# Key pages, gate weights, adaLN pieces and value groups of a hybrid decoder step, moved to other stages

## The chip, the cores and the metric

The kernel runs on one core of a Trainium2 chip. The core has five engines that run their own instruction streams in order: TensorE (PE in the profile; PEld is its loading of weights), VectorE (DVE), ScalarE (ACT), GpSimd (POOL) and SyncE (SP), which here issues nearly all transfers. The metric is the device time of one launch in microseconds (us), lower is better.

## The reference

One layer of a decoder trunk for a prompt of 512 tokens and 8 samples of one new token each, 520 columns in all, with D = 1024, 16 heads of 64, a feed-forward width of 2816, in f32:

```python
m = adaLN(c)                      # shift1, scale1, gate1, shift2, scale2, gate2
h = RMSNorm(x) * (1 + scale1) + shift1
z = h @ w_in                      # rg_x | rg_gate | q | k | v | forget logits | gate A | gate B
ya = (rg_lru(conv4(rg_x)) * gelu(rg_gate)) @ w_proj_a
yb = attend(q, k, v, logf) @ w_proj_b
x = x + gate1 * ((sigmoid(gA) * ya + sigmoid(gB) * yb) @ w_o)
x = x + gate2 * SwiGLU(RMSNorm(x) * (1 + scale2) + shift2)
y = RMSNorm(x)
```

The prompt attends to itself; each sample attends to 1024 past tokens, which lie in 8 pages of 128 tokens per sample, found by a page table: 64 pages of keys and 64 of values, [128 tokens, 16 x 64] f32 each. The logits of the past are q . k / 8 plus a sum of log forget values; a softmax runs over them and the sample's own new token. The outputs are y, the new k, v and log forget values, and the states of the convolution and the recurrence.

## The kernel before

Activations lie with features on partitions: a tile is [128 features, 520 tokens], in two halves of 260 columns. Each f32 operand of a product is split into a rounded part and a rest (hi and lo, the latter the difference), and a product is three matmuls: hi x hi, lo x hi, hi x lo. For weights a chunk `wraw` (up to 1 MB, 2 buffers) is loaded by SP, ACT casts `whi` from it (L210), and DVE subtracts `wlo` (L211), with 3 buffers each, so the split units run ahead of PE by at most three. `begin` (L227) is called for each unit of 128 output features; it ticks the side work, loads chunks and splits weights as far ahead as a budget allows.

The stages in order: a start (RMSNorm, the first adaLN third, the first half of q); the **q stage**, one turn of a loop (L782) for each of q0 to q7; the **recurrent branch** (xr, ga, gb, gr: convolution, RG-LRU, gates); k0, v0 and the **projection pa**, eight units; eight **attention blocks**, each for two heads of the prompt (scores `sc`, softmax, transposes `ptt`, products `po`) with the k and v products of the next block; then pb, wo and the feed-forward part.

Side work is put between by hand-written tables. The units are numbered n = 0 (q6), 1 (q7), 2 and 3 (xr0, xr1), 4 and 5 (ga0, ga1), 6 and 7 (gb0, gb1) and so on; 33 ends the recurrent branch, and 41 ends pa.

- **Key pages.** `KEYS[n]` says how many pages unit n loads (L605 and L606: SP reads the page's number from the table, then issues the transfer into a buffer `pg`, of a pool that the adaLN weights `araw` and the row `qb` share). `qb` is a sample's q row, broadcast to all partitions from `qtd` in memory, where it was written after all q's transposes (`qt`, L763). Two ticks after a page's load DVE multiplies it by `qb` (L636) and sums over each head's 64 columns into `S` (L637); four pages (`POOL_KEYS`) are multiplied on POOL (L624). `KEYS` begins at n = 4 and gives 52 pages; 12 more come in attention blocks 0 to 2 (`KEYS_AT`).
- **The past's softmax** (`past_softmax`, L664 to L700) runs for each pair of samples, a step every two ticks, once its 16 pages are summed: maxima, `dg` (DVE), `lgm` (PE, L685), exponentials, `lgs` (PE).
- **Values** (`pv`, L718): a group is two value pages and four matmuls on PE. 8 groups are due in units of the recurrent branch and pa, 25 slots in attention.
- **Forget values**: POOL gathers the past's into `lfp`, which takes one of the two `wraw` buffers; `past_turn` transposes it (`lft`, PE), once after q6 and once after q7.
- **adaLN pieces** (`ada_piece`, L290): two transfers `araw` of 512 KB and four matmuls on PE each. Pieces 0 to 5 of the second third go with q2 to q7, 6 with xr0 and 7 with xr1.
- **Gate weights** of the RG-LRU (`gw`, `gws`, L823 to L857): loaded in `conv`, cast and subtracted behind each xr.
- **Decay rows** in attention (`decay_rows`): SP broadcasts a head's row `fb` from `ftd`; ACT copies half of it to `fm` (L1063), POOL adds a mask to the parts.

Of the kernel before, what the change touches and what calls it, by code (L numbers as in the profile page):

```python
# [8 lines left out]
F32 = mybir.dt.float32  # L9
F32R = mybir.dt.float32r  # L10
# [54 lines left out]
def kernel(ctx, tc, xT, par, gates, b_f, cst, cse, own, cache_k, cache_v, cache_lf, pt,  # L65
# [103 lines left out]
    def flush():  # L169
        while stores:  # L170
# [3 lines left out]

    KEYS = dict(zip(range(4, 42), (2, 2, 3, 2, 0, 0, 0, 1, 2, 2, 2, 1, 0, 0, 0, 1, 2, 2, 2, 2, 0, 1, 1, 1, 2, 2, 2, 3,
                                   1, 1, 2, 1, 2, 1, 2, 1, 2, 1)))
    VALUES = (21, 23, 25, 27, 29, 31, 35, 39)
    POOL_KEYS = (41, 44, 47, 50)
# [260 lines left out]
    def q_weights(fh, raw, ko, i):  # L439
# [5 lines left out]
        for k in range(0, 4, 2 if (fh, i) == (0, 0) else 4):  # L445
            ks = slice(k, k + 2 if (fh, i) == (0, 0) else 4)
            act.copy(hi[:, ks], src[:, ks])
            dve.tensor_tensor(lo[:, ks], src[:, ks], hi[:, ks].bitcast(F32), ALU.subtract)
        for n in range(2):
            qw[fh, i + n] = [(hi[:, k, 128 * n:128 * n + 128], lo[:, k, 128 * n:128 * n + 128]) for k in range(4)]  # L450

    def q_matmuls(fh, i, j, k, b):
        hi, lo = qw[fh, i][k]
        ah, al = h[4 * fh + k]
        t0, t1 = HALVES[j]
        for m, (wt, at) in enumerate(((hi, ah), (lo, ah), (hi, al))):
            pe.matmul(b[:, :HALF], lhsT=wt, rhs=at[:, t0:t1], start=k == 0 and m == 0, stop=k == 3 and m == 2)  # L457

# [141 lines left out]

    def page_load(cache, s, j):
        pg = pgp.tile([128, D], F32, name="pg", tag="pg")
# [10 lines left out]

    def key_page(s, j):
        if s == 0 and j == 0:
            S.extend(slot("S", 512) for _ in range(2))
        if j == 0:
            t = pgp.tile([128, D], F32, name="qb", tag="pg")
# [4 lines left out]
        if late:  # L623
            pool.tensor_tensor(pg, pg, qb[0], ALU.mult)  # L624
        pend.append([0, s, j, pg, None if late else qb[0]])

    def key_sums():
        for p in pend:
            p[0] += 1
        while pend and pend[0][0] >= 2:  # L630
            _, s, j, pg, q = pend.pop(0)
            r = s // 2
            c = 256 * (r % 2) + 32 * j + H * (s % 2)
            with tc.issue_after(state["last"].ins):
                if q is not None:
                    dve.tensor_tensor(pg, pg, q, ALU.mult)  # L636
                dve.tensor_reduce(S[r // 2][:, c:c + H], pg.rearrange("p (h d) -> p h d", d=DH), AX.X, ALU.add)  # L637
            summed[r] += 1
# [7 lines left out]

    keys_todo = [(s, j) for s in range(NS) for j in range(NPAGE)]
    chains = []
# [125 lines left out]
    def past_conv():  # L774
# [4 lines left out]
        dve.tensor_reduce(conv_past, t, AX.X, ALU.add)  # L779

    ready = []
    for i in range(KT):  # L782
# [15 lines left out]
        if i == 3:  # L798
            split_upto(0)
        if i == 4:  # L800
            past_load()
# [19 lines left out]

    gate_raw = {}

    def gate_load(i):
        if i not in gate_raw:
            gate_raw[i] = slot("gw", 256)
            sp.dma_start(gate_raw[i], gates[i])
        return gate_raw[i]

    def conv(i):  # L830
        gr = gate_load(i)
        if i + 1 < KT:
            gate_load(i + 1)
        xr, xc = slot("xr"), slot("xc")
# [19 lines left out]
        def close():  # L854
            gw = slot("gws", 512, F32R)
            act.copy(gw[:, :256], gr)
            dve.tensor_tensor(gw[:, 256:], gr, gw[:, :256].bitcast(F32), ALU.subtract)  # L857
            del gate_raw[i]
            lru[i].update(xs=split("xc", xc), gw=gw)

# [78 lines left out]
    for i in range(0, KT, 2):  # L939
        conv(i)  # L940
        if i == 0:
            q_done(*q_last)
            past_sums(0)
            ada_piece(1, 6)
        else:
            both(lru_root, i - 2)
            gelu(i - 2)
            lru_scan(i - 2)
        conv(i + 1)
        if i == 0:  # L950
            past_sums(1)
            ada_piece(1, 7)
            ada_copy(1)
        else:
            gelu(i - 1)
            lru_scan(i - 1)
            both(lru_mul, i - 2)
            both(lru_g, i - 2)
        if i < 6:
            gate_a(i)  # L960
            lru_gates(i)
            if i == 0:
                ada_end(1)
# [91 lines left out]
    def decay_rows(i):  # L1055
        for hd in (2 * i, 2 * i + 1):
# [5 lines left out]
            fm = slot("fm", 512)  # L1062
            act.copy(fm[:, :256], fb[:, :256])  # L1063
            for dst, b in ((f0[:, 128 * a:128 * a + 128], 0), (fm[:, 384:], 1), (fm[:, 256:384], 2), (fb[:, 384:], 3)):
# [469 lines left out]
```

## Time and profile before

| | us |
|---|---|
| median of 3 runs | 1085.18 (1083.56 to 1087.83) |
| the profiled execution's own time | 1084.21 |
| its span | 1082.1 |
| PE busy in the span | 1035.1 |
| q stage | 52 to 96 |
| recurrent branch | 96 to 296 |
| k0, v0 and pa | 296 to 369 |
| attention blocks | 369 to 585 |
| pb, wo, feed-forward part | 585 to 1082 |

Times inside the run are read from the trace of one profiled execution and count from the start of its span. Matmuls are pipelined: the 48 matmuls of a unit (two halves of 260 columns) take 5.96 us on PE's chain, though each single one is listed with 0.28. A row of the waits names the instruction that waited, what released it, the total, the number of times and the longest. A row of the chain gives start, duration, engine, result, line and count.

### The profile page before, as it was taken

The page shows a single profiled execution, that of the slowest core. Times are in us where ns is not written, and L with a number is a line of the kernel's source. Part 1 is how long each engine was busy: PE and PEld are TensorE (multiplying, and loading weights), DVE is VectorE, ACT ScalarE, POOL GpSimd, SP SyncE. Part 2 cuts the span into 40 slices and gives each one's busy share as a digit, 9 for nine tenths or more (in the row PEclk, how much of TensorE's full clock was granted, in tenths as well). Part 3 has the DMA queues.
Part 4 walks back from the last instruction along what each step waited for, and adds up shares of the span by engine and source line. Part 5 has one row for each costly group of instructions (what it writes and reads, how often), then busy time and mean ns, then how long its engine had stood idle before and what let it go on. Part 6 is the DMA issues. An engine that isn't in the chain of part 4 may idle for free.

```text
span 1082.1 us, 20877 instructions
## 1 busy us (share of the span) xinstructions
PE 1035.1 (96%) x8210; PEld 955.1 (88%) x8210; DVE 663.6 (61%) x1158; ACT 498.9 (46%) x983; POOL 161.3 (15%) x249
## 2 busy tenths in 40 slices
PE   4999999999979989998999999999999999999996
PEld 2888999999879967777778989999999999999995
DVE  5434799978899888875655455843343333433354
ACT  4423585857831466686775234533312332222352
POOL 1102010100032424452420002400000000000013
PEclk9999999999999989998999999999999999999998
DMA  9795776679779988898875773223323422323212
GB/s 335 264 346 197 237 268 188 213 247 294 245 220 334 295 282 248 288 295 267 237 248 194 256 278 86 72 79 81 115 78 88 109 79 95 101 79 99 77 60 80
DMA packets 164996, 206.94 MB, mean 191 GB/s; under 512 B 9490, under 2 KB 125730, under 8 KB 164834
## 3 DMA queue, kind: packets, MB, share of 16 engines
q1 hardware_dynamic: 161170, 198.70, 57.9%
q10 hardware_dynamic: 3648, 6.39, 1.6%
q8 instruction: 64, 1.05, 0.4%
q0 software_dynamic: 80, 0.52, 0.2%
q14 instruction: 34, 0.28, 0.1%
HBM read 192.49 MB, written 13.09 MB: 190 GB/s over the span
## 4 chain that ended last, share of the span: by engine, by line
PE 81%; DVE 7%; DMA 5%; ACT 2%; issue 2%; POOL 1%; SPq 1%; POOLq 0%; DVEq 0%
PE fiu L245 11%; PE fig L245 11%; PE fo L245 10%; PE gb L245 4%; PE xr L245 4%; PE pb L245 4%; PE ga L245 4%; PE v L245 4%; PE pa L245 3%; PE gr L245 3%; PE wo L245 3%; DMA fb<-ftd 2%; PE k L245 2%; PE pv L718 2%; PE qp L457 2%
## 5 line engine op out<-in xcount | busy, mean ns | idle before, releaser
L211 DVE TENSOR_TENSOR wlo<-wraw,whi 128x1024 fp32r<-128x1024 f32 (+1 forms) x131 | 163.1, 1245 | 161.3 <-ACT whi L210 161.3
L210 ACT CAST whi<-wraw 128x1024 fp32r<-128x1024 f32 (+1 forms) x131 | 136.4, 1041 | 209.3 <-PE fo L245 74.5
L245 PE MATMUL fiu<-h2h,whi 128*128 128x260 f32 x320 | 90.9, 284 | 0.0
L245 PE MATMUL fiu<-h2l,whi 128*128 128x260 f32 x320 | 90.6, 283 | 0.0
L245 PE MATMUL fig<-h2l,whi 128*128 128x260 f32 x320 | 90.3, 282 | 0.0
L245 PE MATMUL fiu<-h2h,wlo 128*128 128x260 f32 x320 | 90.3, 282 | 0.0
L245 PE MATMUL fig<-h2h,wlo 128*128 128x260 f32 x320 | 90.3, 282 | 0.0
L245 PE MATMUL fig<-h2h,whi 128*128 128x260 f32 x320 | 90.2, 282 | 0.0
L245 PE MATMUL fo<-ach,whi 128*128 128x260 f32 x292 | 82.7, 283 | 0.0
L245 PE MATMUL fo<-ach,wlo 128*128 128x260 f32 x292 | 82.5, 283 | 0.0
L245 PE MATMUL fo<-acl,whi 128*128 128x260 f32 x292 | 82.2, 282 | 0.0
L637 DVE TENSOR_REDUCE S<-pg 128x16 f32<-128x1024 f32 x64 | 76.4, 1210 | 1.3 <-POOL pg L624 1.0
L327 POOL TENSOR_TENSOR ss<-ss,sq 128x260 f32<-128x260 f32 x18 | 13.6, 757 | 420.3 <-ACT sq L326 419.8
L636 DVE TENSOR_TENSOR pg<-pg,qb 128x1024 f32<-128x1024 f32 x60 | 72.4, 1224 | 0.2 <-DMA pg<-in_cache_k_dram 0.2
L245 PEld LDWEIGHTS fiu<-h2h,wlo 128*128 128x128 f32 x320 | 60.5, 189 | 0.0
L245 PEld LDWEIGHTS fiu<-h2l,whi 128*128 128x128 f32 x320 | 60.3, 188 | 0.0
L245 PEld LDWEIGHTS fig<-h2h,whi 128*128 128x128 f32 x320 | 60.2, 188 | 0.0
L245 PEld LDWEIGHTS fig<-h2l,whi 128*128 128x128 f32 x320 | 60.2, 188 | 0.0
L245 PEld LDWEIGHTS fig<-h2h,wlo 128*128 128x128 f32 x320 | 60.2, 188 | 0.0
L245 PEld LDWEIGHTS fiu<-h2h,whi 128*128 128x128 f32 x320 | 60.2, 188 | 0.0
L245 PEld LDWEIGHTS fo<-acl,whi 128*128 128x128 f32 x292 | 55.0, 188 | 0.0
L245 PEld LDWEIGHTS fo<-ach,wlo 128*128 128x128 f32 x292 | 54.9, 188 | 0.0
(382 smaller groups left out, 3377.0 us busy)
## 6 DMA issues: line engine op xcount, KB each, us to landing
pg<-in_cache_k_dram SPq DMA_DIRECT2D x64, 512.0 KB, 5.3
pg<-in_cache_v_dram SPq DMA_DIRECT2D x64, 512.0 KB, 5.4
araw<-in_ada_w_dram SPq DMA_DIRECT2D x48, 512.0 KB, 7.3
wraw<-in_w_fi_dram SPq DMA_DIRECT2D x44, 512.0 KB, 5.1
wraw<-in_w_in_dram SPq DMA_DIRECT2D x34, 512.0 KB, 6.3
wraw<-in_w_in_dram SPq DMA_DIRECT2D x11, 1024.0 KB, 6.9
wraw<-in_w_fo_dram SPq DMA_DIRECT2D x8, 1024.0 KB, 5.3
x<-in_xT_dram SPq DMA_DIRECT2D x16, 260.0 KB, 6.2
```

The costliest lines, as they stand in the source:

```text
L210: state["act"] = act.copy(hi[:, :k1 - k0], src)
L211: state["last"] = dve.tensor_tensor(lo[:, :k1 - k0], src, hi[:, :k1 - k0].bitcast(F32), ALU.subtract)
L245: state["mm"] = pe.matmul(out[:, :HALF], lhsT=wt[k], rhs=at, start=k == 0 and m == 0, stop=k == nk - 1 and m == 2)
L327: eng.tensor_tensor(acc[:, t0:t1], acc[:, t0:t1], q_, ALU.add)
L457: pe.matmul(b[:, :HALF], lhsT=wt, rhs=at[:, t0:t1], start=k == 0 and m == 0, stop=k == 3 and m == 2)
L636: dve.tensor_tensor(pg, pg, q, ALU.mult)
L637: dve.tensor_reduce(S[r // 2][:, c:c + H], pg.rearrange("p (h d) -> p h d", d=DH), AX.X, ALU.add)
L718: pe.matmul(pv[0][32 * gq:32 * gq + 32, :], lhsT=pw[r][:, c:c + 32], rhs=pgs[gq // 2][:, 512 * hf:512 * hf + 512], start=j == 0, stop=j == ...
```

## The change

- Keys of samples 0 and 1 come as halves by heads: an item is a pair of pages, of each 512 of its 1024 columns (two transfers of 256 KB into one buffer, 16 items, the first half of the heads first), with half a `qb`. Their product and sum run over a pair of halves at once. Six items are loaded in the q stage with q3, q4 and q5 (two each), two more with q6; `KEYS` now begins at n = 0 and gives 58 pages' worth, none is left for attention. `q_done` of q3 runs in q3's own turn, so that the first half of q is written to `qtd` before the items of the first half.
- `POOL_KEYS` are unchanged in their numbers, so these four pages come earlier.
- `VALUES` has 12 units (8 before), attention 20 slots (25 before).
- The gate weights of all eight i are loaded and split with q5 and q6, four each (`gate_split`).
- adaLN pieces 0 to 3 stay with q2 to q5; 4 goes with xr0 and 5 with xr1; 6 goes with xr2 and 7 with xr3; what follows the last piece moves with it.
- The copy to `fm` is done by POOL.

By the tables the keys loaded up to n = 33 are 53 pages' worth (40 before), up to n = 5 are 14 (4 before).

```diff
-    KEYS = dict(zip(range(4, 42), (2, 2, 3, 2, 0, 0, 0, 1, 2, 2, 2, 1,
...
-    VALUES = (21, 23, 25, 27, 29, 31, 35, 39)
+    KEYS = dict(zip(range(42), (2, 0, 0, 0, 3, 3, 3, 2, 0, 1, 1, 1, 2, 2, 2, 1,
...
+    VALUES = (17, 19, 21, 23, 25, 27, 29, 31, 33, 35, 37, 39)
...
-        if 4 <= n < 42:
+        if n < 42:
             tick(KEYS[n], n in VALUES)
...
-        loads.append(sp.dma_start(pg, cache[bass.ds(r, 1)].rearrange("a p c -> (a p) c")))
+        loads.append(sp.dma_start(pg, cache[bass.ds(r, 1), :, c0:c1].rearrange("a p c -> (a p) c")))
...
+    def key_halves(s, j, half):
+        if not S:
             S.extend(slot("S", 512) for _ in range(2))
+        pg = pgp.tile([128, 2, 512], F32, name="pg", tag="pg")
+        for a in range(2):
+            page_load(cache_k, s, j + a, pg[:, a], 512 * half, 512 * half + 512)
+        if j == 0:
+            t = slot("qb", 512)
+            sp.dma_start(t, qtd[s:s + 1, 512 * half:512 * half + 512].partition_broadcast(128))
+            qb[0] = t
+        pend.append([0, s, j, pg, qb[0], half])
...
+                if half is not None:
+                    b, c = 8 * (r % 2) + j, H * (s % 2) + 8 * half
+                    dve.tensor_tensor(pg, pg, q.unsqueeze(1).to_broadcast([128, 2, 512]), ALU.mult)
+                    dve.tensor_reduce(S[r // 2].rearrange("p (b c) -> p b c", c=32)[:, b:b + 2, c:c + 8],
+                                      pg.rearrange("p j (h d) -> p j h d", d=DH), AX.X, ALU.add)
...
-    keys_todo = [(s, j) for s in range(NS) for j in range(NPAGE)]
+    keys_todo = [(s, j, half) for half in range(2) for s in range(2) for j in range(0, NPAGE, 2)]
+    keys_todo += [(s, j) for s in range(2, NS) for j in range(NPAGE)]
...
+    def gate_split(i):
+        gr = slot("gw", 256)
+        sp.dma_start(gr, gates[i])
+        gw = gws[i] = slot("gws", 512, F32R)
+        act.copy(gw[:, :256], gr)
+        dve.tensor_tensor(gw[:, 256:], gr, gw[:, :256].bitcast(F32), ALU.subtract)
...
+        if i in (5, 6):
+            for n in range(4 * i - 20, 4 * i - 16):
+                gate_split(n)
...
-        if i >= 2:
+        if 2 <= i < 6:
             ada_piece(1, i - 2)
+        if i == 3:
+            q_done(*ready.pop())
+        if i in (3, 4, 5):
+            tick(2, 0)
...
-            ada_piece(1, 6)
+            ada_piece(1, 4)
         else:
+            if i == 2:
+                ada_piece(1, 6)
...
-            act.copy(fm[:, :256], fb[:, :256])
+            pool.tensor_copy(fm[:, :256], fb[:, :256])
...
-    KEYS_AT = [(1, 1, 1, 1)] * 3 + [(0, 0, 0, 0)] * 5
...
-    VALUES_AT = [(1, 1, 0, 1)] * 6 + [(1, 1, 1, 1), (1, 1, 1, 0)]
+    VALUES_AT = [(1, 1, 0, 1), (1, 0, 0, 1)] * 3 + [(1, 1, 0, 1), (1, 1, 0, 0)]
...
-        tick(KEYS_AT[i][part], VALUES_AT[i][part])
+        tick(0, VALUES_AT[i][part])
```

How it moves instructions, first on SP, which issues the transfers in this order. Before, from the end of q5 to the first unit of the recurrent branch (`wraw` in the fourth row is the chunk of ga0 and ga1, that in the last row the chunk of gb0 and gb1; the chunk of xr0 and xr1 stands eight rows further up; the last `araw` but one belong to q6 and q7):

```order
L295 DMA araw<-in_ada_w_dram 128x1024 x3
L762 DMA qd<-q 128x520
L562 DMA fld<-fl 16x520
L186 DMA wraw<-in_w_in_dram 128x8x256
L295 DMA araw<-in_ada_w_dram 128x1024
L605 TENSOR_LOAD ptb
L605 ISA x2
L605 TENSOR_LOAD ptb
L605 ISA x2
L762 DMA qd<-q 128x520
L827 DMA gw<-in_gates_dram 128x256 x2
L186 DMA wraw<-in_w_in_dram 128x8x256
```

Now, at the same place; the first of the two `wraw` is the chunk of xr0 and xr1, behind the eighth key item, and the second that of ga0 and ga1, which takes the buffer of `lfp`; the three `araw` behind them belong to pieces 4 and 5:

```order
L608 DMA pg<-in_cache_k_dram 128x512
L186 DMA wraw<-in_w_in_dram 128x8x256 x2
L784 DMA qd<-qp 128x520
L807 DMA gw<-in_gates_dram 128x256
L784 DMA qd<-q 128x520
L295 DMA araw<-in_ada_w_dram 128x1024
L807 DMA gw<-in_gates_dram 128x256
L295 DMA araw<-in_ada_w_dram 128x1024 x2
L807 DMA gw<-in_gates_dram 128x256
```

Both chunks, half of the gate weights and the adaLN pieces now stand close together behind the pages, where before the chunks and pieces were spread over the stage.

On PE, around the first unit of the recurrent branch (xr_0), before:

```order
L763 MATMUL qt_718<-cs,q 8x128
L373 MATMUL lft_1049<-cs,lfp 128x64 x8
L298 MATMUL ada_666<-araw,silc 32x512 x4
L245 MATMUL xr_0_1093<-hh,whi 128x260
L245 MATMUL xr_0_1093<-hh,wlo 128x260
```

and now:

```order
L785 MATMUL qt_770<-cs,q 8x128
L373 MATMUL lft_1267<-cs,lfp 128x64 x8
L298 MATMUL ada_666<-araw,silc 32x512 x6
L245 MATMUL xr_0_1303<-hh,whi 128x260
L245 MATMUL xr_0_1303<-hh,wlo 128x260
```

The place of ada in the stream is the same, but it now works on three `araw` and not two, and on those that SP issues behind the chunk that waits for lft.

On SP again, further up, around the end of q3. The second `araw` of the stage stands behind four half pages and the fourth `qd` (that of q3), where before it stood behind the second `qd`:

```order
L608 DMA pg<-in_cache_k_dram 128x512
L784 DMA qd<-qp 128x520
L295 DMA araw<-in_ada_w_dram 128x1024
L792 DMA qtd<-qt 8x512
L295 DMA araw<-in_ada_w_dram 128x1024
L625 DMA qb<-qtd 128x512
L607 TENSOR_LOAD ptb
```

The row of q for sample 0 (`qb`) follows directly on the write of the first half of q (`qtd`).

More of the change, by code (lines that the diff above doesn't have):

```diff
@@ L446, in q_weights @@
             ks = slice(k, k + 2 if (fh, i) == (0, 0) else 4)
-            act.copy(hi[:, ks], src[:, ks])
-            dve.tensor_tensor(lo[:, ks], src[:, ks], hi[:, ks].bitcast(F32), ALU.subtract)
+            state["act"] = act.copy(hi[:, ks], src[:, ks])
+            state["last"] = dve.tensor_tensor(lo[:, ks], src[:, ks], hi[:, ks].bitcast(F32), ALU.subtract)
         for n in range(2):
@@ L612, with key_page @@
     summed = [0] * 4
-    def key_page(s, j):
-        if s == 0 and j == 0:
+    def key_halves(s, j, half):
+        if not S:
             S.extend(slot("S", 512) for _ in range(2))
+        pg = pgp.tile([128, 2, 512], F32, name="pg", tag="pg")
[6 more added lines that the diff above has]
+        pend.append([0, s, j, pg, qb[0], half])
+    def key_page(s, j, half=None):
+        if half is not None:
+            return key_halves(s, j, half)
         if j == 0:
@@ L624, in key_page @@
             pool.tensor_tensor(pg, pg, qb[0], ALU.mult)
-        pend.append([0, s, j, pg, None if late else qb[0]])
+        pend.append([0, s, j, pg, None if late else qb[0], None])
     def key_sums():
@@ L630, in key_sums @@
         while pend and pend[0][0] >= 2:
-            _, s, j, pg, q = pend.pop(0)
+            _, s, j, pg, q, half = pend.pop(0)
             r = s // 2
@@ L634, in key_sums @@
             with tc.issue_after(state["last"].ins):
-                if q is not None:
-                    dve.tensor_tensor(pg, pg, q, ALU.mult)
-                dve.tensor_reduce(S[r // 2][:, c:c + H], pg.rearrange("p (h d) -> p h d", d=DH), AX.X, ALU.add)
+                if half is not None:
+                    b, c = 8 * (r % 2) + j, H * (s % 2) + 8 * half
+                    dve.tensor_tensor(pg, pg, q.unsqueeze(1).to_broadcast([128, 2, 512]), ALU.mult)
+                    dve.tensor_reduce(S[r // 2].rearrange("p (b c) -> p b c", c=32)[:, b:b + 2, c:c + 8],
+                                      pg.rearrange("p j (h d) -> p j h d", d=DH), AX.X, ALU.add)
+                else:
+                    if q is not None:
+                        dve.tensor_tensor(pg, pg, q, ALU.mult)
+                    dve.tensor_reduce(S[r // 2][:, c:c + H], pg.rearrange("p (h d) -> p h d", d=DH), AX.X, ALU.add)
             summed[r] += 1
@@ L854, in close @@
         def close():
[L855 to L859, printed above, removed]
+            lru[i].update(xs=split("xc", xc), gw=gws.pop(i))
         defer(0, close)
@@ L961 @@
             lru_gates(i)
-            if i == 0:
+            if i == 2:
                 ada_end(1)
```

28 lines of the change are left out of this document (12 added, 16 removed).

## The prediction

> **What bounds the kernel now.** I read the page first: busy times, then the stretches of the span, then who waits for whom, then the chain around the places that the change touches. On the page:
>
> ```profile
> PE 1035.1 (96%) x8210; PEld 955.1 (88%) x8210; DVE 663.6 (61%) x1158; ACT 498.9 (46%) x983; POOL 161.3 (15%) x249
> PE   4999999999979989998999999999999999999996
> ```
>
> TensorE (PE) is the bound: nothing that leaves another engine shortens the run unless PE waits for it. What can be won is PE's idle time and the time in which its clock was halved. The change ends its edits before 585 us, so I cut the span there. Columns: stretch, length, busy PE, PEld, DVE, ACT, POOL (instructions), granted PE clock, DMA share, GB/s.
>
> ```profile
> 52.00:96.00 44.00, 44.00 (x347) 35.87 (x347) 18.44 (x54) 13.61 (x26) 6.36 (x19) 1.00 0.84 290
> 96.00:140.00 44.00, 44.00 (x344) 39.82 (x345) 29.77 (x55) 21.68 (x42) 3.74 (x11) 1.00 0.68 213
> 140.00:189.00 49.00, 49.00 (x411) 49.00 (x410) 47.63 (x58) 34.06 (x61) 3.29 (x4) 1.00 0.72 228
> 189.00:241.00 52.00, 52.00 (x428) 49.56 (x426) 47.48 (x62) 35.58 (x63) 3.41 (x5) 1.00 0.69 224
> 241.00:282.00 41.00, 41.00 (x329) 37.10 (x328) 35.98 (x48) 29.46 (x54) 1.98 (x4) 1.00 0.82 266
> 282.00:322.00 40.00, 34.18 (x273) 31.11 (x271) 35.14 (x46) 25.53 (x41) 6.97 (x8) 0.99 0.74 251
> 322.00:369.00 47.00, 47.00 (x365) 45.95 (x365) 45.62 (x69) 15.26 (x34) 12.52 (x10) 0.94 1.00 313
> 369.00:420.00 51.00, 43.77 (x303) 35.65 (x302) 42.98 (x70) 27.08 (x66) 23.14 (x28) 0.90 0.89 285
> 420.00:470.00 50.00, 48.60 (x334) 38.51 (x334) 43.18 (x85) 34.23 (x86) 24.30 (x28) 0.97 0.90 282
> 470.00:506.00 36.00, 32.50 (x226) 28.02 (x226) 20.84 (x55) 23.33 (x61) 11.27 (x21) 0.91 0.99 287
> 506.00:585.00 79.00, 77.58 (x592) 64.34 (x590) 47.63 (x117) 59.66 (x137) 21.07 (x32) 1.00 0.74 236
> ```
>
> The q stage (52 to 96) and the recurrent stage (96 to 282) lose nothing: PE is busy all the time at full clock. All losses lie behind 282. Idle is length less PE busy; what the clock costs is (1 - clock) x length. 282 to 322: 5.8 + 0.4; 322 to 369: 0 + 2.8; 369 to 420: 7.2 + 5.1; 420 to 470: 1.4 + 1.5; 470 to 506: 3.5 + 3.2; 506 to 585: 1.4 + 0. The sum is **32.3 us**, the most that the change can win. Who was late there, from the waits (line that waited, releaser, total, times, longest) and the chain of the first of them:
>
> ```profile
> PE ptt L1105 <- DVE ksB L1005: 5.3, 5, 2.8
> PE lgm L685 <- DVE dg L680: 4.6, 1, 4.6
> PE lgm L685 <- DVE pl L1110: 2.9, 1, 2.9
> ```
> ```profile
> ACT fm L1063 <- DMA fb<-ftd: 22.7, 12, 4.6
> ```
> ```profile
> 314.10 2.26 DVE S L637 x2
> 316.36 1.37 DVE pg L636
> ...
> 319.09 1.20 DVE wlo L211
> 320.29 0.48 DVE dg L680
> ...
> 320.91 1.15 PE lgm L685 x2
> ```
>
> The 4.6 us stall is VectorE (DVE) work on key pages (S, pg) standing in front of the softmax over the past; the 2.9 us one is the same chain's next round. The ptt stall is ScalarE (ACT), which stands in order at fm for the decay rows (fb) and comes late with what ksB needs.
>
> **What the change removes.** A key page costs DVE one product and one sum:
>
> ```profile
> L637 DVE TENSOR_REDUCE S<-pg 128x16 f32<-128x1024 f32 x64 | 76.4, 1210 | 1.3 <-POOL pg L624 1.0
> L636 DVE TENSOR_TENSOR pg<-pg,qb 128x1024 f32<-128x1024 f32 x60 | 72.4, 1224 | 0.2 <-DMA pg<-in_cache_k_dram 0.2
> ```
>
> That is 1.21 + 1.22 = 2.43 us. A pair of halves has as many elements as one page, so I price it alike; DVE's total stays. Twelve pages, 29 us of DVE, leave attention, and the softmax chains over the past run earlier. I take as gone: both losses of 282 to 369 (9.0), those of 369 to 420 (12.3) and, since fm's copy moves to POOL and ACT no longer stands at fb, those of 470 to 506 (6.7): 28.0. A transfer still ends some of these waits, so I leave one half-clock stretch of 2.8 standing: **-25.2**. The small losses of 420 to 470 and 506 to 585 (4.3) I leave. Ends: all 32.3, or, if ACT was not the cause of ptt, 28.0 - 6.7 - 2.8 = 18.5.
>
> The copies on POOL are no term: POOL is busy 24.3 of 50 us at its fullest. If that cover goes, the 16 rows come late, and the price is again the 6.7. Four value groups leave attention for the recurrent stage; PE does them in either place, so nothing changes.
>
> **What it adds in the q stage.** Here PE lost nothing, so each wait counts in full. At the first unit of the recurrent branch, before:
>
> ```profile
> 93.89 1.03 PE lft L373 x8
> 94.92 0.99 PE ada L298 x8
> 95.92 5.95 PE xr L245 x48
> ```
> ```profile
> 94.22 0.33 SPq L762 DMA_DIRECT2D qd<-q  x1
> 94.61 0.92 SPq L827 DMA_DIRECT2D gw<-in_gates_dram  x2
> 95.63 0.38 SPq L186 DMA_DIRECT2D wraw<-in_w_in_dram  x1
> ```
> ```profile
> L295 SPq DMA_DIRECT2D araw<-in_ada_w_dram x13: 372/398/1150, 56.2 to 87.9; - x13
> ...
> DMA to landing us min/median/max: 4.6/6.2/8.5
> ```
>
> Now the queue of SyncE (SP) has two 1 MB chunks of weights here, and the second goes into the buffer of lfp, so it waits for the last lft. Behind it stand qd, gw, qd, araw, gw, araw, araw; and PE's next row after lft is ada on these three araw, with xr behind it. From 94.9: 0.38 + 0.33 + 0.46 + 0.33 + 0.40 + 0.46 + 0.80 = 3.2, so the last is issued at 98.1 and lands 6.2 later, at 104.3. Six ada take 12 passes at 0.125 (0.99 over 8), 1.5 us, 1.0 of which can be done before the last lands; PE idles 104.3 + 0.5 - 94.9 - 1.5 = **8.4 us** (6.8 to 10.7 by the ends of the row). A wait of that length will halve the clock; 322 to 369 shows what one such stretch cost behind a 4.6 us stall: 2.8 (0 if no window falls on it): **+2.8**.
>
> Further ahead, ada behind q4 takes an araw which is now issued behind qd of q3, past four half pages:
>
> ```profile
> 65.25 0.33 SPq L762 DMA_DIRECT2D qd<-qp  x1
> ```
> ```profile
> 69.04 1.83 PE ada L298 x10
> ```
>
> 65.25 + 0.33 = 65.6, and 0.1 to the next issue; landing at 65.7 + 6.2 = 71.9, where PE wants it at 69.0: **+2.9** (1.3 to 5.2). Together 14.1.
>
> The Trainium skill, "TensorE: Matmul & The Clock Gate", in "Why this matters for your kernels", says that idle gaps of PE above some 3 us drop the clock to half, one window of idle being enough. By that rule the 2.9 us wait pays only itself and the sum stands. The trace is stricter: in 470 to 506 the longest wait was 2.8, with 3.5 us idle in all, and the clock was 0.91. By this row the 2.9 us wait would cost up to 3.2 more and the sum would be 1079; I keep that for the upper end.
>
> **What DVE must carry earlier.** By the key table 13 more pages are loaded by the end of the recurrent stage (53 for 40), 13 x 2.43 = 31.6 us; ten of them (24.3 us) are summed up by the unit gb1, so in 52 to 140 at the old times. DVE has 25.6 + 14.2 = 39.8 us free there, and PE's waits of 14 us add as much. The other 7.3 meet 49 + 52 + 41 - 131.1 = 10.9 us free in 140 to 282. It fits on the average, but tightly: at 140 to 189 DVE is busy 47.6 of 49. Bounds: 0, and 8.5 if eight of the thirteen (19.4 us) come only behind 140 (19.4 - 10.9). I take **+2**, near nothing, as the rows show PE not waiting where DVE was 97% busy. The gate weights' splits are moved, not added; ACT is 14 of 44 busy there and covers them; without that cover a split is some 0.4 us each on ACT.
>
> **The sum**, against the profiled execution of 1084.2 us (span 1082.1): +8.4 + 2.8 + 2.9 + 2 - 25.2 = -9.1, so 1075.1. It ran 1.0 below the median of 1085.18, so in terms of the median **1076**.
>
> **The rivals.**
> *The gain is given back.* The ptt stall was the transfer's own lateness, not ACT's order: fb rows took long to land whoever copies them, and the 22.7 us ACT stood there ended mostly without PE waiting. Then 18.5 is won for 14.1 + 2.8 (a second half-clock stretch) + 2: +0.4, no change, 1086. Against it: the keys leave the same queues. Chance 0.22.
> *DVE becomes the bound of the recurrent stage*, slower than before. The halves wait for the first half of q to go out to memory and come back as a row for all partitions; every page stands in order on DVE in front of the weights' splits (wlo). If more than the 10.9 us free behind 140 slips past it, PE waits for wlo from then on. If all 31.6 do, that is 20.7 instead of 2: 1076 + 18.7 = 1095. Against it: PE's own waits give DVE 14 us. Chance 0.16.
> *The waits in the q stage are short* (6.8 + 1.3, no halved clock) and attention runs nearly clean (30): -21.9 with nothing for DVE, so 1063. For it: the queues were 84% busy in 52 to 96, so the last araw may land in the least time of its row. Chance 0.17.
> *The transfers bind the q stage.* From qd of q0 to the last of the three araw the queue now moves 12.8 MB; at the 290 GB/s of 52 to 96 that is 44 us from about 55, 99 us, as in the sum; at the 213 of the next row, 60 us and 115: 10 more, 1086. Chance 0.04. The Trainium skill, "DMA: Bandwidth & Descriptors", in "Bandwidth", speaks for this rival: it wants 1 MiB a transfer for three quarters of the peak, and the halves are 256 KB. The rows do not bear it out in landing times:
>
> ```profile
> pg<-in_cache_k_dram SPq DMA_DIRECT2D x64, 512.0 KB, 5.3
> wraw<-in_w_in_dram SPq DMA_DIRECT2D x11, 1024.0 KB, 6.9
> x<-in_xT_dram SPq DMA_DIRECT2D x16, 260.0 KB, 6.2
> ```
>
> Size hardly shows there, with several in flight.
>
> **How the numbers follow.** The forecast itself has 0.41. The range goes from the short waits with all losses gone (-32.3 + 8.1 = -24.2, 1061) to 18.5 won for the long ends and half of DVE's bound (10.7 + 5.2 + 5.6 + 4.3 = 25.8), +7.3, 1093; DVE's worst lies beyond. 0.5% (5.4 us) is about what a measurement of this kernel can tell from no change. Faster (below 1079.8): most of the forecast (0.37) and the short waits (0.17), 0.54. Slower (above 1090.6): DVE as the bound and a little, 0.18. The rest, 0.28, is the same.
>
> **What would show it.** Right: PE idle 8 us between the last lft and xr, ended by araw, with a halved clock behind it; some 3 us at ada behind q4; lgm's wait of 4.6 gone; 369 to 585 (as the same work) with under 8 us lost. Wrong: wlo among the releasers of PE between xr2 and the first pa; PE waiting at ptt for ksB as before; or no wait at lft.

## The result, and the profile after

| | before | changed |
|---|---|---|
| median, us (4 runs each, same chip) | 1086.02 | 1101.95 |
| span of the profiled execution | 1082.1 | 1099.5 |

The ratio is 1.0154, 95% interval 1.0126 to 1.0182: 16 us slower, where 9 faster was forecast. First the page of the changed kernel, whose lines answer to the two at the head of the prediction (busy time, then PE's busy tenths in 40 slices):

```profile
PE 1041.4 (95%) x8210; PEld 954.5 (87%) x8210; DVE 669.4 (61%) x1158; ACT 499.5 (45%) x972; POOL 156.1 (14%) x265
PE   4996899999998998999999999999999999999996
```

The same 8210 matmuls keep PE busy 6.3 us longer, and the weak slices now stand further left, in the first quarter. To see where the time went I cut both traces at the same instructions: the first matmul of ga0, of k0, of k1 and of gb6. Each row is a stage; columns as in the prediction. Before:

```profile
52.00:113.30 61.30, 61.30 (x468) 48.99 (x467) 28.77 (x85) 21.57 (x43) 10.10 (x29) 1.00 0.79 267
113.30:296.00 182.70, 182.70 (x1501) 175.38 (x1498) 159.80 (x200) 126.67 (x220) 8.68 (x13) 1.00 0.74 239
296.00:368.80 72.80, 66.98 (x519) 63.84 (x518) 71.29 (x103) 26.73 (x54) 19.29 (x17) 0.95 0.89 282
368.80:562.10 193.30, 179.75 (x1259) 146.07 (x1257) 141.77 (x290) 126.55 (x315) 77.57 (x105) 0.95 0.87 268
```

and the changed kernel:

```profile
52.00:134.00 82.00, 67.30 (x449) 51.38 (x447) 44.61 (x87) 23.18 (x47) 9.50 (x29) 0.90 0.81 258
134.00:333.20 199.20, 192.60 (x1536) 178.73 (x1535) 178.31 (x228) 131.44 (x222) 19.29 (x17) 0.99 0.79 245
333.20:408.60 75.40, 71.05 (x537) 64.01 (x536) 65.59 (x93) 24.02 (x48) 10.75 (x16) 0.95 0.81 255
408.60:579.20 170.60, 164.71 (x1219) 138.22 (x1217) 118.52 (x268) 123.07 (x303) 70.87 (x117) 0.98 0.83 253
```

The stages differ by +20.7, +16.5, +2.6 and -22.7 us. Part of that is work that moved: two adaLN pieces (2.0 us) left the first stage for the second, two value groups came into the second and two into the third (2.1 each), and four left the fourth (4.2). Without it:

| stage | lost (+) or won (-) | forecast |
|---|---|---|
| to ga0 (q stage, xr0, xr1) | +22.7 | +14.1 |
| ga0 to k0 (recurrent branch) | +12.4 | +2 |
| k0 to k1 (pa) | +0.5 | -9.0 |
| k1 to gb6 (attention) | -18.5 | -16.2 |
| sum | +17.1 | -9.1 |

The gain in attention is there. The price in front of it is more than twice what was forecast, and pa gained nothing. What PE waited for in the changed kernel (total, times, longest):

```profile
PE ada L298 <- DMA araw<-in_ada_w_dram: 12.9, 3, 9.1
...
PE pa L245 <- DVE gl L279: 4.4, 2, 3.6
PE xr L245 <- ACT fl L562: 3.5, 1, 3.5
PE gate L897 <- ACT gate L898: 2.5, 1, 2.5
PE pv L740 <- DMA pg<-in_cache_v_dram: 2.5, 1, 2.5
PE ga L245 <- ACT tA L955: 2.4, 1, 2.4
...
PE ptt L1132 <- DVE ksB L1032: 1.1, 1, 1.1
```

The lgm waits (7.5 us before) are gone, and ptt fell from 5.3 to 1.1. New are waits for araw, for ACT, and in pa for gl, which now takes about as long as the lgm wait that stood there before (4.4 us for 4.6).

The 9.1 us wait is the one that was forecast as 8.4. But it was not the last thing that xr0 waited for. The chain of the changed kernel, from the last lft to xr0, in order of time:

```profile
97.69 1.05 PE lft L373 x8
...
98.76 6.22 DMA wraw<-in_w_in_dram
...
105.08 1.04 ACT whi L210
106.12 0.32 ACT gws L809
...
108.15 1.15 DVE wlo L211
...
109.35 0.38 SPq L186
...
109.83 5.71 DMA gw<-in_gates_dram
...
115.57 0.41 ACT gws L809
115.97 0.38 ACT fl L562
...
116.40 3.70 PE xr L245 x17
```

SP stands at the second weight chunk until lft is done (98.76). ACT casts that chunk, DVE subtracts (a sum over key halves, 1.1 us, comes first), and only then is there a buffer for the third chunk (109.35). The gate weights' last load stands behind the third chunk on SP (109.83). On ACT the casts of the gate weights stand in front of fl, and xr0 waits for fl. ACT stood idle for 8.3 us in front of three of these casts (in brackets the idle time before an instruction, and what ended it):

```profile
108.25 0.41 ACT L809 CAST gws<-gw 128x256 fp32r<-128x256 f32 x1 [1.83 <-DMA gw<-in_gates_dram]
111.35 0.41 ACT L809 CAST gws<-gw 128x256 fp32r<-128x256 f32 x1 [2.69 <-DMA gw<-in_gates_dram]
115.57 0.41 ACT L809 CAST gws<-gw 128x256 fp32r<-128x256 f32 x1 [3.81 <-DMA gw<-in_gates_dram]
115.88 0.82 ACT L562 ACTIVATE fl<-pfs,bf 16x260 f32<-16x260 f32 x2
```

So the gate weights are the end of this chain, and the adaLN pieces are beside it. But the pieces were not free: PE's stream has them ahead of xr0, and they held PE until 112.9.

```profile
107.86 5.04 PE L298 MATMUL ada<-araw,silc 128*32 128x512 f32 x12 [9.13 <-DMA araw<-in_ada_w_dram]
116.40 0.58 PE L245 MATMUL xr<-hh,whi 128*128 128x260 f32 x1 [3.50 <-ACT fl L562]
```

In this order, a fl that came in time would have let xr0 start 3.5 us earlier and no more.

### The profile page after: what moved, and what is told of

It is laid out like the page before. It is cut to its first block, busy times and chain, and to the rows that moved or that the text cites. A ratio compares the mean times of both kernels' runs of the same rounds, so it can differ in the third digit from the quotient of the medians.

```text
span 1099.5 us, 21007 instructions
## 1 busy us (share of the span) xinstructions
PE 1041.4 (95%) x8210; PEld 954.5 (87%) x8210; DVE 669.4 (61%) x1158; ACT 499.5 (45%) x972; POOL 156.1 (14%) x265
## 3 DMA queue, kind: packets, MB, share of 16 engines
q8 instruction: 64, 1.05, 0.4%
## 4 chain that ended last, share of the span: by engine, by line
PE 74%; DVE 10%; DMA 7%; ACT 4%; issue 3%; POOL 1%; SPq 1%; POOLq 0%; DVEq 0%; ACTq 0%
PE fig L245 10%; PE fiu L245 10%; PE fo L245 10%; PE pb L245 4%; PE pa L245 4%; PE k L245 3%; PE gb L245 3%; DMA wraw<-in_w_in_dram 3%; PE v L245 3%; PE ga L245 3%; PE xr L245 3%; PE wo L245 3%; PE pv L740 3%; DVE wlo L211 2%; PE po L1166 2%
## 5 line engine op out<-in xcount | busy, mean ns | idle before, releaser
L211 DVE TENSOR_TENSOR wlo<-wraw,whi 128x1024 fp32r<-128x1024 f32 (+1 forms) x131 | 160.4, 1226 | 153.8 <-ACT whi L210 153.8
L245 PE MATMUL fig<-h2l,whi 128*128 128x260 f32 x320 | 90.4, 283 | 0.0
L245 PE MATMUL fiu<-h2l,whi 128*128 128x260 f32 x320 | 90.4, 283 | 0.0
L245 PE MATMUL fig<-h2h,wlo 128*128 128x260 f32 x320 | 90.4, 282 | 0.0
L245 PE MATMUL fiu<-h2h,wlo 128*128 128x260 f32 x320 | 90.4, 282 | 0.0
L658 DVE TENSOR_REDUCE S<-pg 128x16 f32<-128x1024 f32 x48 | 57.6, 1211 | 0.2
L657 DVE TENSOR_TENSOR pg<-pg,qb 128x1024 f32<-128x1024 f32 x44 | 55.5, 1271 | 0.0
L245 PEld LDWEIGHTS fo<-ach,whi 128*128 128x128 f32 x292 | 55.0, 188 | 0.0
```

Source lines behind the costliest of these rows:

```text
L211: state["last"] = dve.tensor_tensor(lo[:, :k1 - k0], src, hi[:, :k1 - k0].bitcast(F32), ALU.subtract)
L245: state["mm"] = pe.matmul(out[:, :HALF], lhsT=wt[k], rhs=at, start=k == 0 and m == 0, stop=k == nk - 1 and m == 2)
```

## The experiments

Each ratio is against the kernel before on the same chip, with its interval. In the table, the time of the first matmul of some units in the profiled execution:

| run | median | ratio | xr0 | ga0 | k0 | k1 | gb6 |
|---|---|---|---|---|---|---|---|
| before | 1086.0 | 1 | 95.9 | 113.3 | 296.0 | 368.8 | 562.1 |
| changed | 1102.0 | 1.0154 | 116.4 | 134.0 | 333.2 | 408.6 | 579.2 |
| e1 pieces back | 1101.3 | 1.0138 (1.0111 to 1.0164) | 115.6 | 135.7 | 331.5 | 407.1 | 577.8 |
| e2 gates back | 1092.3 | 1.0051 (1.0033 to 1.0069) | 98.9 | 120.0 | 325.1 | 400.3 | 571.7 |
| e3 both back | 1101.5 | 1.0134 (1.0112 to 1.0155) | 99.7 | 127.2 | 335.0 | 410.6 | 581.7 |
| e25 gate loads only | 1091.3 | 1.0036 (1.0016 to 1.0056) | 106.1 | 126.1 | 327.9 | 403.3 | 573.8 |
| e21 pieces ahead | 1105.1 | 1.0161 (1.0120 to 1.0201) | 124.3 | 141.6 | 342.0 | 418.1 | 589.2 |
| e7 no q keys | 1086.2 | 0.9992 (0.9981 to 1.0004) | 94.8 | 113.6 | 313.1 | 383.6 | 563.6 |
| e14 late scan on e7 | 1074.5 | 0.9888 (0.9853 to 0.9924) | 94.6 | 113.1 | 304.9 | 374.7 | 552.4 |
| e17 late scan on e2 | 1085.7 | 0.9986 (0.9969 to 1.0003) | 101.3 | 122.7 | 319.7 | 394.0 | 566.4 |
| e10 16 pages on POOL, e7 | 1089.4 | 1.0014 (1.0000 to 1.0028) | 94.6 | 113.2 | 321.0 | 391.5 | 569.3 |
| e12 16 pages on POOL, e2 | 1094.0 | 1.0036 (1.0011 to 1.0060) | 100.4 | 121.9 | 326.1 | 403.3 | 574.3 |
| e4 fm alone | 1079.6 | 0.9922 (0.9900 to 0.9944) | 94.5 | 112.0 | 294.7 | 366.9 | 557.1 |
| e15 changed, fm on ACT | 1125.2 | 1.0349 (1.0312 to 1.0386) | 116.6 | 134.9 | 333.4 | 409.5 | 602.6 |
| e8 split pieces | 1094.4 | 1.0055 (1.0038 to 1.0072) | 101.8 | 121.6 | 304.3 | 375.4 | 574.7 |
| e18 late keys on POOL, e4 | 1082.1 | 0.9958 (0.9940 to 0.9977) | 96.0 | 113.4 | 296.2 | 368.5 | 561.4 |
| e19 four keys earlier, e4 | 1072.6 | 0.9868 (0.9833 to 0.9903) | 96.1 | 113.6 | 297.0 | 366.1 | 549.3 |
| e23 eight keys earlier, e4 | 1077.2 | 0.9915 (0.9884 to 0.9947) | 95.7 | 113.1 | 303.4 | 375.9 | 556.5 |
| e24 keys spread | 1068.5 | 0.9831 (0.9809 to 0.9853) | 94.6 | 112.5 | 297.7 | 366.3 | 543.9 |

### The q stage: pieces, gates, keys

e1 puts the adaLN pieces back, e2 the gate weights, e3 both:

```diff
# e1
-        if 2 <= i < 6:
+        if i >= 2:
             ada_piece(1, i - 2)
...
# e2
...
-            lru[i].update(xs=split("xc", xc), gw=gws.pop(i))
+            gw = slot("gws", 512, F32R)
+            act.copy(gw[:, :256], gr)
+            dve.tensor_tensor(gw[:, 256:], gr, gw[:, :256].bitcast(F32), ALU.subtract)
+            del gate_raw[i]
+            lru[i].update(xs=split("xc", xc), gw=gw)
```

> The changed kernel with the adaLN pieces at their old places (0 to 5 with q2 to q7, 6 and 7 with xr0 and xr1). Theory (the loss is made on SP's queue in the q stage): the 9.1 us wait for araw in front of xr0 and the half clock behind it (about 2.4) go, and so does the 1.7 us wait for araw behind gr0; the pieces now wait for page buffers in the q stage instead, some 3 us. Time 1089 to 1094 (changed kernel 1102). Rival (VectorE is the bound of the recurrent stage because 13 more pages are summed there): the waits only change their place, time within 3 of 1102.

> The changed kernel with the gate weights loaded and split per unit as before. Theory: the 3.5 us wait of xr0 for ScalarE, which stood at a gws cast for its transfer, goes with its half clock (1.6), and the araw come some 1 us earlier. Time 1095 to 1098. Rival (VectorE bound): within 3 of 1102.

> The changed kernel with both adaLN pieces and gate weights as before; key halves, value groups and the copy on POOL as in the changed kernel. Theory: the sum of both, 1082 to 1088, a little below or at the kernel before. Rival (VectorE bound): above 1097.

The theory missed e1 and e3, and e2 won more than it said. With the pieces back (e1) nothing changed: the pieces still land behind the chunk (the longest wait for araw is 8.1), and xr0 is where it was. With only the gates back (e2) xr0 starts at 98.9 and 9.7 us are won. This win has two parts that the run does not separate: fl is no longer late, and the order of PE's stream is another one, for in e2 the pieces stand behind xr0 and not ahead of it:

```profile
107.73 1.05 PE L298 MATMUL ada<-araw,silc 128*32 128x512 f32 x4 [0.95 <-DMA araw<-in_ada_w_dram]
110.36 1.05 PE L298 MATMUL ada<-araw,silc 128*32 128x512 f32 x4 [1.57 <-DMA araw<-in_ada_w_dram]
```

With both back (e3) xr0 starts as early, but then PE waits for the pieces between xr0 and ga0 (4.2 us at once, with a half-clock stretch, and the pieces in halves between the units), and the gain is gone. So with key items in the q stage the pieces are better late, as the change has them; it is the move of the gate weights that cost, with the order that came with it. Two more runs go into this. e25 leaves the gate loads where the change put them and moves only the cast and the subtraction back:

```diff
-        gw = gws[i] = slot("gws", 512, F32R)
-        act.copy(gw[:, :256], gr)
-        dve.tensor_tensor(gw[:, 256:], gr, gw[:, :256].bitcast(F32), ALU.subtract)
+        gws[i] = gr
...
```

> The changed kernel in which the gate weights are still loaded with q5 and q6, but cast and subtracted behind each xr as before. Theory (the q stage's loss comes from ScalarE, which stands in order at the casts until the late gate transfers land, so that fl and the banks of xr0 behind it wait; the adaLN wait lies beside it): xr0 starts below 102 and the time is that of the run with the gates as before, 1090 to 1095. Rival (the loads on SP's queue make it, wherever the cast stands): within 3 of 1102, xr0 above 112.

The time is the theory's, 1091.3; xr0, at 106.1, lies between the two. ACT starts the part of fl that xr0 waits for at 105.66, not at 115.97, so ACT's in-order stand at the casts is shown as the larger part of fl's lateness. That xr0 could follow it has again to do with PE's order: here too the pieces stand behind xr0, at 116.5, and do not hold it. What is left of the wait is this:

```profile
PE xr L245 <- ACT fl L562: 7.1, 1, 7.1
```

There fl still stands behind the cast of the second chunk on ACT, whose load SP could issue only after lft (98.98); in e2 ACT does fl at 90.4, before that cast. e21 loads pieces 4 and 5 in q5's turn, ahead of the chunks:

```diff
...
+        if i == 5:
+            ada_load(1, 4)
+            ada_load(1, 5)
```

> The changed kernel with the four transfers of adaLN pieces 4 and 5 issued in q5's turn, ahead of the two weight chunks of which the second waits for the last lft. Theory (SP stands 7 us at that chunk, and the pieces behind it make the 9.1 us wait and most of the half clock in front of xr0): that wait is below 2 us, the wait of xr0 for ScalarE behind the gate weights stays: 1088 to 1093. Rival (key pages fill the transfers and buffers, so the pieces are late wherever they stand): within 3 of 1102, the wait only moved.

```profile
PE xr L245 <- ACT fl L572: 22.7, 1, 22.7
```

The wait for araw in front of xr0 is gone, and the run is no faster. Everything on SP behind these loads came later, the gate loads too (the last at 118.3, not at 109.8), and xr0 waits 22.7 us for fl. So taking away the 9.1 us wait, the longest, wins nothing as long as the gate weights' chain stands beside it. e7 has gates and pieces as before and no key items in the q stage:

```diff
...
-        if i in (3, 4, 5):
-            tick(2, 0)
...
-        tick(0, VALUES_AT[i][part])
+        tick(1 if i == 0 else 0, VALUES_AT[i][part])
```

> As the run with both put back, and no key items in the q stage: eight pages' worth of items later (four in units xr0 and xr1, four in attention block 0). Theory: nothing is lost in the q stage, xr0 starts within 1 us of 95.9; attention keeps most of its gain of about 20; time 1066 to 1076, below the kernel before. Rival (VectorE bound in the recurrent stage): the same key work in a shorter stretch, PE waits for wlo or for splits of activations there by 10 us or more, time 1083 or above.

The first half of the theory held: xr0 starts 1.0 us earlier than before (e4, further down, which changes nothing up to there, starts it 1.4 earlier, so this difference says nothing). The second did not: k0 comes 17 us late (2.1 of it are the two value groups), and the run is even with the kernel before.

### The recurrent branch

Against e7 stood the rival that VectorE has too much to do there. In e7 DVE is nearly full from 140 to 220, but not here:

```profile
220.00:240.00 20.00, 15.81 (x111) 13.15 (x110) 12.94 (x21) 10.27 (x21) 0.32 (x2) 0.91 0.64 185
```

and its own waits say why:

```profile
DVE fcs L580 <- DMA lf<-lfd: 6.4, 1, 6.4
```

DVE stands in order at the running sum over the log forget values, which go out to memory and come back, and their transfers are late. e14 moves only that sum, from xr3's block to gb5:

```diff
         sp.dma_start(lf, lfd)
+
+    def forget_sums():
         fcs = slot("fcs", NP, parts=H)
...
             if i == 2:
                 log_forget()
+            if i == 4:
+                forget_sums()
```

> As the run without key items in the q stage (1086), with VectorE's running sum over the log forget values (fcs) moved from behind xr3's block to behind gb5, so that VectorE does not stand at the transfer lf (6.4 us there, 7.6 to 7.7 in the runs with 16 pages on POOL and with the gates put back). Theory (a wait in order on VectorE, which the late transfers of the log forget values make, holds the splits in front of ga5): PE's 4.2 us idle and 1.7 of half clock between ga4 and xr6 go: 1079 to 1082. Rival (VectorE has simply too much to do): within 3 of 1086.

It won 12 us, more than expected: k0 moved from 313.1 to 304.9, and k1 to gb6 took 177.7 us, not 180.0. e17 does the same on e2:

> The changed kernel with the gate weights as before (1092) and the running sum over the log forget values behind gb5 (12 us in the run without q keys). Theory (VectorE stood 7.6 us at the transfer lf there): 1080 to 1085. Rival (its recurrent stage is late for other reasons): within 3 of 1092.

It won 6.6 us and ends 0.7 outside the theory's range. Its k0 comes 5.4 us earlier although its xr0 was 2.4 later. In the changed kernel itself the chain that ends in the 2.4 us wait at ga5 runs over the same two transfers (232.5 to 241.6), but DVE came to fcs late too and stood there for 0.7 only. So this wait is shown for e7 and e2, not for the changed kernel. Is it also DVE's work? Two runs move the product of every third unsplit page to POOL (16 pages, not 4), on e7 and on e2:

```diff
-    POOL_KEYS = (41, 44, 47, 50)
+    POOL_KEYS = tuple(range(17, 64, 3))
```

> As the run without key items in the q stage (1086), with 16 instead of 4 pages multiplied on POOL (every third of the unsplit pages). Theory (VectorE is the bound of the recurrent stage: in that run it is busy 20 of 20 us in three of four stretches from 140 to 220): 9 to 12 pages of that stage leave 1.2 us of VectorE each, PE's idle 9.3 and half clock 3.4 between the first ga and the first pa fall to 3 or less: 1074 to 1078. Rival (the order on SP's queue and on ScalarE makes these waits): within 3 of 1086.

> The changed kernel with the gate weights as before (1092) and 16 instead of 4 pages multiplied on POOL. Theory (VectorE bound): about 10 of the 17.6 us that this kernel loses between ga0 and gr7 against the kernel before come back, 1080 to 1084. Rival (SP's and ScalarE's order): within 3 of 1092.

Neither won: e10 is 3.1 us slower than e7 and e12 1.7 slower than e2, so neither theory held (the rivals' range fits e12 and misses e10 by 0.4). In e10 DVE is no longer full (16.86, 16.00, 12.20 of 20 from 180 to 240), yet the wait at fcs grew to 7.7 and k0 came later. With that wait in the way, taking work off DVE bought nothing. It is no clean trial of DVE's load, though: a product takes 2.6 us on POOL (the median; up to 6.5) for 1.2 on DVE, and DVE's sums waited 2.3 us for POOL.

### Attention: fm and the keys

e4 is the kernel before with one line changed; e15 is the changed kernel with that line undone:

```diff
-            act.copy(fm[:, :256], fb[:, :256])
+            pool.tensor_copy(fm[:, :256], fb[:, :256])
```

> The kernel before with only the copy to fm on POOL. First theory (that of the prediction: ScalarE, standing at fb for fm, makes the ptt wait of 470 to 506): 5 to 7 us faster, 1079 to 1081, the ptt waits gone. Rival (the transfer of fb and the key work set that stretch): within 2 us of before, and the ptt wait of 2.8 is still there.

> The changed kernel with the copy to fm back on ScalarE. Theory (that copy alone gave the kernel before 8.5 us, and gives the changed kernel as much): 1108 to 1112, with ptt waits for ksB again. Rival (with no key pages in attention ScalarE has room to stand at fb): within 3 of 1102, so that the attention stage's gain is the keys'.

e4 won 8.5 us, near the 6.7 of the prediction. In its trace the stretch that answers to 470 to 506 lost almost nothing, where PE was busy for 32.5 us at a clock of 0.91 before:

```profile
468.00:504.00 36.00, 35.84 (x266) 29.96 (x262) 25.81 (x63) 26.26 (x68) 16.56 (x31) 1.00 0.93 263
```

But k1 to gb6 as a whole is only 3.1 us shorter: earlier in it the wait for lgm grew from 2.9 to 5.2 us and that for lgs from 1.0 to 2.3. e15 lost 23 us against the changed kernel, far beyond both expectations. From k1 to gb6 it takes 193.1 us, as the kernel before, although it has no key page there and four value groups less. Its waits in 400 to 620 begin with

```profile
PE ptt L1132 <- DVE ksB L1032: 12.6, 11, 3.7
```

where the changed kernel had 1.1. So attention's gain needs both moves: the keys out alone win nothing, fm alone about 3 of the 193 us in its trace, both 18.5 (22.7 with the four value groups that left).

e18 leaves the pages in attention and has six of the twelve multiplied by POOL; e19 and e23 take four and eight of the twelve out of attention, and put them into recurrent units that loaded none (e19 into units 8, 10, 16 and 18; its expectation names 20 and 22 for the last two):

```diff
# e18, on e4
-    POOL_KEYS = (41, 44, 47, 50)
+    POOL_KEYS = (41, 44, 47, 50, 52, 54, 56, 58, 60, 62)
# e19, on e4
-    KEYS = dict(zip(range(4, 42), (2, 2, 3, 2, 0, 0, 0, 1, 2, 2, 2, 1, 0, 0, 0, 1,
...
+    KEYS = dict(zip(range(4, 42), (2, 2, 3, 2, 1, 0, 1, 1, 2, 2, 2, 1, 1, 0, 1, 1,
...
-    KEYS_AT = [(1, 1, 1, 1)] * 3 + [(0, 0, 0, 0)] * 5
+    KEYS_AT = [(1, 1, 1, 1)] * 2 + [(0, 0, 0, 0)] * 6
# e23, on e4
+    KEYS = dict(zip(range(4, 42), (2, 2, 3, 2, 1, 1, 1, 1, 2, 2, 2, 1, 1, 1, 1, 1, 2, 2, 2, 2, 2, 1, 1, 1, 2, 2, 2, 3,
...
+    KEYS_AT = [(1, 1, 1, 1)] + [(0, 0, 0, 0)] * 7
```

> The kernel before with the copy to fm on POOL (1079.6) and six of attention's twelve key pages multiplied on POOL too. Theory (VectorE's key work in front of the past's softmax makes the lgm waits of attention, 9.6 us with their half clock): VectorE has 7 us less there, 1072 to 1077. Rival (the chain waits for transfers of pages, whoever multiplies): within 3 of 1079.6.

> The kernel before with the copy to fm on POOL and four key pages taken out of attention block 2 and put into units 8, 10, 20 and 22 of the recurrent stage, whose VectorE has 10.9 us free from 140 to 282. Theory (four pages, 9.7 us, still fit there): the recurrent stage loses less than 2 us and attention gains some 4: 1074 to 1078. Rival (each page put there costs PE about 1 us or more, as nine pages cost some 13 in the run without q keys): 1079 to 1085.

> The kernel before with the copy to fm on POOL and eight (not four) key pages taken from attention into the recurrent stage. Theory (VectorE's 10.9 us free from 140 to 282 are the limit, four pages filled 9.7 of it): the next four, 9.7 us, find no room, PE loses 6 to 9 us there and attention gains 4: 1074 to 1078, slower than the run with four (1072.6). Rival (there is room, since VectorE's waits of 10 to 19 us for whi are slack too): 1066 to 1071.

e18 is for its rival: multiplying elsewhere does not help. e19 and e23 bracket the room on DVE. With four pages (9.7 us of DVE) xr0 to k0 takes 200.9 us, 200.1 in the kernel before, and the run is 7 us faster than e4, more than its theory said. The next four make k0 6.3 us later, and the run is 4.6 slower than e19. The limit lies between 9.7 and 19.4 us, where the windows of the kernel before show 10.9 free from 140 to 282.

### The moves that paid, together

e24 has fm on POOL, gates, pieces and values as before, the key halves from xr0 on (none in the q stage), four pages in attention and the late sum:

```diff
...
+    KEYS = dict(zip(range(42), (0, 0, 2, 2, 2, 2, 3, 2, 1, 0, 1, 1, 2, 2, 2, 1, 1, 0, 1, 1, 2, 2, 2, 2, 0, 1, 1, 1, 2, 2, 2, 3,
+                                1, 1, 2, 1, 2, 1, 2, 1, 2, 1)))
...
```

> The kernel before with the copy to fm on POOL, key halves from xr0 on (none in the q stage), four pages in attention (block 0), and the late running sum; gates, adaLN pieces and values as before. Four more pages than in the run with 1072.6 go to units xr0 and xr1, where VectorE has 14.2 us free (96 to 140). Theory (pages are free as long as VectorE has room in their stretch): 1066 to 1071. Rival (what is left in attention does not hang on keys): within 3 of 1072.6.

1068.5, 1.7% faster than the kernel before and the fastest of all. The late sum is in it too, so what it wins over e19 is not the pages' alone. Its first two stages, cut at 113.0 and 296.0 (ga0 starts at 112.5, k0 at 297.7):

```profile
52.00:113.00 61.00, 61.00 (x466) 48.91 (x466) 27.89 (x67) 21.23 (x40) 10.38 (x29) 1.00 0.83 280
113.00:296.00 183.00, 180.97 (x1486) 173.91 (x1485) 177.63 (x237) 127.96 (x221) 6.54 (x15) 1.00 0.84 256
```

The q stage is clean again, and PE is idle for 2.0 us only in the recurrent branch, with DVE busy 177.6 of 183.

### What a piece costs on PE

In the changed kernel the two transfers of most pieces stand apart, and so a piece's four matmuls (eight passes in the trace) run as two and two. A piece before, and the two halves of one after:

```profile
60.63 1.07 PE L298 MATMUL ada<-araw,silc 128*32 128x512 f32 x8
```
```profile
83.84 1.05 PE L298 MATMUL ada<-araw,silc 128*32 128x512 f32 x4
...
85.62 1.05 PE L298 MATMUL ada<-araw,silc 128*32 128x512 f32 x4
```

Four passes take as long as eight. e8 puts the halves of pieces apart in the kernel before, with nothing else changed:

```diff
...
-            for gg in range(2):
+            def mms(g2=g2, raw=raw):
+                for gg in range(2):
...
+            if which != 1 or g2 == 0:
+                mms()
+            else:
+                later_half.append(mms)
```

> The kernel before with the two halves of most adaLN pieces of the second third apart on TensorE: the second half's two matmuls run between the halves of the following product, six more groups in all, the same matmuls and transfers. Theory (the four matmuls of a piece, which write four different strips of columns, run side by side, so a group costs about 1.0 us whether it has two or four): six times 1.0, 6 us slower, with the loss before the first ga. Rival (cost goes by the number of passes, 0.125 each): no change, within 1 us.

It is 6.1 us slower for six groups more, as the theory says. (In its trace ga0 comes 8.3 us later, and 1.2 of that is there before the first piece.) In the changed kernel six of the eight pieces of this third, the last six, run in halves: four groups more up to ga0 and two behind it. The prediction priced them by passes.

## Why the prediction was wrong

By stages the forecast was off by 8.6 us up to ga0, 10.4 in the recurrent branch, 9.5 in pa and 2.3 the other way in attention, 26.2 in all. Step by step:

- **PE as the bound, and the losses behind 282**: right. The losses in attention were won (18.5 for 16.2).
- **fm**: right in mechanism, and in size for the stretch from 470 to 506 (e4). e15 shows that it carried attention's gain, together with the keys.
- **"I take as gone: both losses of 282 to 369 (9.0)"**: wrong. The stage lost 0.5 more than before. The lgm wait went, and a wait for gl of the same size with a half-clock stretch took its place. The chain of the trace in front of gl is DVE's own work from 334 on (DVE is busy for all of 333.2 to 346.0): the recurrent branch, with more pages in it, now ended late on DVE. The step took a stall away without asking what is late next.
- **The wait in front of xr0** (8.4, measured 9.1) and **the one behind q4** (2.9, measured 2.1): right as waits. Behind the first came 3.5 us more for fl, and behind the second a half-clock stretch that the sum had left out (1.7).
- **"The gate weights' splits are moved, not added; ACT is 14 of 44 busy there and covers them"**: this step, a term put at nothing, failed. An average of ACT's busy time says nothing of what stands behind a cast that waits for a transfer. The casts stood in order in front of fl, and the last load stood behind a chunk that waited for a buffer. In the changed kernel this made the 3.5 us on top of the pieces' wait. Undoing that one move wins 9.7 us of the 15.9 (e2), the other order on PE included.
- **Pieces at 0.125 a pass**: wrong; a group costs about 1.0 us whether it has four passes or eight (e8). The four groups more up to ga0 are about 4 us.
- **"DVE must carry earlier", +2**: mis-sized; the stage lost 12.4, more than the prediction's upper bound of 8.5, though 2.1 of it are pieces in halves and 1.7 a wait for araw. The room on DVE was right as a sum (e19, e23). What it left out is order: an engine that is full on the average meets transfers that are late (fcs, e14), and stands.
- **The rivals**: the slower one had DVE as the bound behind halves that slip. DVE's work was late at gl, and in e23; the delays at SP and ACT in front of xr0 were in no rival.
- **The signs**: those for "right" came out nearly all (9.1 us at araw, 2.1 behind q4, lgm's wait gone), and none of those for "wrong" did. No sign looked at the terms that failed.

Open: which of the 12.4 us of the changed kernel's recurrent branch hang on late transfers and which on DVE's work was not taken apart there. No run has the gates back with the pieces still ahead of xr0, so how much of e2's win is fl and how much PE's order stays open. Why both back (e3) is 9 us slower than the gates alone is read from its araw waits and not tried by itself.

## What to carry to other kernels

A load that is moved earlier is moved past everything on its queue, and its consumer past everything on its engine: follow each moved instruction to what stands behind it, on both, before costing it at nothing. The wait that the profile names longest need not be the last one at its place; the chain shows what else ends there, and taking the wait away shows what it is worth. An edit can also change the order of a stream that it does not touch: compare the orders before giving a win to the edit alone. Where four small matmuls share the array, keep them together, and load what they need with one landing.

## What the runs showed of the hardware

Matmuls that write different strips of 32 rows of the result run side by side: 1.05 us for four passes and 1.07 for eight. PE's clock fell to half after a shorter wait than the prediction's sum counted with. In the changed kernel a single idle of 2.1 us, behind q4, was followed by this stretch:

```profile
64.00:71.70 7.70, 5.62 (x43) 3.52 (x41) 2.71 (x5) 1.82 (x3) 0.38 (x2) 1.00 0.85 296
71.70:75.20 3.50, 3.50 (x19) 2.79 (x18) 0.95 (x1) 0.00 (x0) 0.00 (x0) 0.51 0.58 187
```

The prediction had left that stretch out of its sum by the Trainium skill, "TensorE: Matmul & The Clock Gate", "Why this matters for your kernels", whose bound for such gaps is some 3 us. The trace does not agree: 3.5 us ran at half clock, which cost 1.7.
